# Each tile streams its own weights, with the two tiles in flight about a third of a layer apart

One step of a two-layer decoder, on the 8 NeuronCores of one Trainium2 chip. Each core computes one prompt sequence of 2048 tokens in four tiles of 512, and a sample group of 32 tokens. The metric is the device time of the slowest core, in microseconds.

## The reference

Cut to what matters: the residual stream passes four feed-forwards, a gated linear attention and a dilated window attention. All weights are shared by all tokens; only the recurrence's state and the keys and values go from tile to tile.

```python
# layer 0
x = x + 0.5 * swiglu_ffn(rmsnorm(x, g), w_in, w_out)      # 1024 -> 2*2688 -> 1024
x = x + gla_mixer(rmsnorm(x, g), ...)                     # recurrence over chunks of 64
x = x + 0.5 * swiglu_ffn(rmsnorm(x, g), w_in, w_out)
k, v = shared_kv(x, ...)                                  # k: per-head norm, rotary
# layer 1
x = x + 0.5 * swiglu_ffn(rmsnorm(x, g), w_in, w_out)
x = x + dilated_window_attention(q, k, v) @ w_o           # windows 128, 512, 2048
x = x + 0.5 * swiglu_ffn(rmsnorm(x, g), w_in, w_out)
```

## The kernel before

Weights come as units (fp32 in HBM, converted to bf16 on the way in) through one ring of 16,384 columns, eight units of 2048. A unit is free when all its users have used it: two prompt tiles, and in the first pass the sample tile. The program is written as Python threads; when it is built, a list scheduler with assumed times lays their instructions out in a fixed order for each engine. At run time each engine goes through its own list and waits for the others: on the slowest core before, TensorE's longest such wait in total is for a norm's VectorE outputs, 49.1 us in 16 waits.

```python
DMA_BW = 190e3
...
RING = 16384
ring = A("ring", [128, RING], BF16)
...
def add_unit(p, kind, i, src, n, users=0):                # p: pair of tiles
    u = Unit(src, n, users or (3 if p == 0 else 2), len(order))
...
def weights():
    for k, u in enumerate(order):
        if off + u.n > RING:
            off = 0
        lo, hi = off, off + u.n
        over = [(a, b, o) for (a, b, o) in live if a < hi and b > lo]
        yield need(lambda over=over: all(o.left == 0 for _, _, o in over))
        ...
        yield O(PL, (lambda e, u=u, dst=dst: e.dma_start(out=dst, in_=u.src)), ...)
...
# the scheduler: of the operations that can start about now, the one of lowest rank
m = min(c[0] for c in cands) + self.TIE
th = min((c for c in cands if c[0] <= m), key=lambda c: (c[1][0], c[1][1]))[1]
...
def c_act(n): return 0.11 + n * 0.00083                   # assumed ScalarE us
def c_dve(n, rate=1): return 0.07 + n / (960.0 * rate)    # assumed VectorE us
```

A feed-forward takes 21 units of the first projection ("wfi", 2048 columns, 16 matmuls for a tile) and 8 of the output projection ("wfo", 2688 columns, 21 matmuls).

Of the kernel before, what the change touches and what calls it, by code (L numbers as in the profile page):

```python
# [24 lines left out]
class Sched:  # L25
# [3 lines left out]
    DMA_BW = 190e3  # L29
# [117 lines left out]
class Threads:  # L147
# [10 lines left out]
    def spawn(self, gen, rank):  # L158
        self.seq += 1
        self.live.append([rank, self.seq, gen, None, None])  # L160

    def run(self):
        S = self.S
        while self.live:
            self.live.sort(key=lambda h: (h[0], h[1]))
            moved = False
            for th in list(self.live):
                while th[3] is None:
                    if th[4] is not None:
                        if not th[4]():  # L170
                            break
                        th[4] = None
                        moved = True
                    try:
                        item = next(th[2])
                    except StopIteration:
                        self.live.remove(th)
                        moved = True
                        break
                    moved = True  # L180
                    if item[0] == "op":
                        th[3] = item
                    else:
                        th[4] = item[1]
            cands = [(S.start_of(th[3][1], th[3][3], th[3][4]), th) for th in self.live if th[3] is not None]
            if not cands:
                if moved:
                    continue
                if self.live:
                    def where(g):  # L190
                        out = []
                        while g is not None:
                            if getattr(g, "gi_frame", None) is not None:
                                out.append("%s:%d" % (g.gi_code.co_name, g.gi_frame.f_lineno))
                            g = getattr(g, "gi_yieldfrom", None)
                        return " > ".join(out)
                    raise RuntimeError("deadlock of threads: %s" % [(h[0], where(h[2])) for h in self.live])
                break
            m = min(c[0] for c in cands) + self.TIE
            th = min((c for c in cands if c[0] <= m), key=lambda c: (c[1][0], c[1][1]))[1]  # L200
            _, eng, fn, reads, writes, cost, dma, nbytes = th[3]
            th[3] = None
            S.op(eng, fn, reads, writes, cost, dma, nbytes)
# [93 lines left out]
def build():  # L297
# [23 lines left out]
    RING = 16384  # L321
    ring = A("ring", [128, RING], BF16)
# [86 lines left out]

    units = {}  # L410
    order = []

    def add_unit(p, kind, i, src, n, users=0):
        u = Unit(src, n, users or (3 if p == 0 else 2), len(order))
        u.kind = kind
        units[(p, kind, i)] = u
        order.append(u)

    for p in range(2):
        def ffn_units(f, p=p):  # L420
            for j in range(NF):
                add_unit(p, "fi%d" % f, j, wfi[f * NF + j], 2048)
            for m in range(8):
                add_unit(p, "fo%d" % f, m, wfo[f * 8 + m], 2688)
        ffn_units(0)
        for gi, kind in enumerate(("v", "qk", "r", "o")):
            for i in range(4):
                add_unit(p, kind, i, wgl[gi * 4 + i], 2048)
            if p == 0 and kind == "qk":
                for s in range(4):  # L430
                    src = st_in[s * 4:(s + 1) * 4].rearrange("h p d -> p h d")
                    add_unit(0, "S0", s, src, 2048, 1)
                    add_unit(0, "S0b", s, src, 1024, 1)
        ffn_units(1)
        for i in range(2):
            add_unit(p, "kv", i, wkv[i], 2048)
        ffn_units(2)
        for i in range(3):
            add_unit(p, "wq", i, wqd[i], 2048)
        if p == 0:  # L440
            for s in range(4):
                add_unit(0, "ck", s, ck[s], 3328, 1)
                add_unit(0, "cv", s, cv[s], 3328, 1)
        for i in range(4):
            add_unit(p, "wo", i, wod[i], 1536)
        ffn_units(3)

    NWS = 12

    def weights():  # L450
        live = []
        off = 0
        for k, u in enumerate(order):
            if off + u.n > RING:
                off = 0
# [9 lines left out]
            if u.kind in ("S0", "S0b"):  # L465
                dst = dst.rearrange("p (h d) -> p h d", h=4)
            yield O(PL, (lambda e, u=u, dst=dst: e.dma_start(out=dst, in_=u.src)),  # L467
                    writes=[u.key] + [o.key for _, _, o in over], cost=1.0, dma="w%d" % (k % NWS), nbytes=u.n * 512)
            u.ready = True

    def use(T, kind, i):
        u = units[(T.p, kind, i)]
        yield need(lambda: u.ready)
        return u
# [16 lines left out]

    tiles = []
    for t in range(4):
        T = Tile()
        i = t % 2
        T.nm, T.i, T.p, T.t, T.n, T.rank = "t%d" % t, i, t // 2, t, 512, 10 * t
# [15 lines left out]
    TS.nm, TS.i, TS.p, TS.t, TS.n, TS.rank = "ts", "s", 0, -1, 32, -20  # L512
# [77 lines left out]
    def load_x(T, prev):  # L590
        nq = 4 if T.n == 512 else 1
        for q in range(nq):
            ms = range(q * 8 // nq, (q + 1) * 8 // nq)
            if prev is not None:
# [5 lines left out]
                writes=[xk(T, m) for m in ms], cost=0.1, dma="x%s_%d" % (T.b, q), nbytes=w * 512)  # L600
# [44 lines left out]
    def ffn(T, f, last):  # L645
# [14 lines left out]
        for j in range(NF):  # L660
# [8 lines left out]
            yield mm(g, [(v[:, kt, 0:128], T.h[:, kt, :]) for kt in range(8)], hks(T) + [u.key], bs[0], n)  # L669
            yield mm(up, [(v[:, kt, 128:256], T.h[:, kt, :]) for kt in range(8)], hks(T) + [u.key], bs[-1], n)  # L670
            u.left -= 1
            TH.spawn(post(j, bs, g, up), T.rank - 3)
# [7 lines left out]
        for m in range(8):  # L680
# [9 lines left out]
            TH.spawn(evac(m, b), T.rank - 4)  # L690
# [20 lines left out]
    def gla(T):  # L711
# [30 lines left out]
        TH.spawn(gate(), T.rank - 5)  # L742
# [5 lines left out]
        for hd in range(4):  # L748
            u = yield from use(T, "v", hd)
            v = u.ap.rearrange("p (kt c) -> p kt c", kt=8)  # L750
            for cp in range(2):
# [4 lines left out]
                TH.spawn(vpost(hd, cp, b, either()), T.rank - 3)  # L756
# [24 lines left out]
        for hd in range(4):  # L781
# [7 lines left out]
            TH.spawn(qkpost(hd, bs), T.rank - 4)  # L789
            if hd % 2:  # L790
                TH.spawn(recur(T, hd // 2), T.rank - 5)
# [39 lines left out]
        TH.spawn(rms_all(), T.rank - 5)  # L831
        for hd in range(4):
            u = yield from use(T, "r", hd)
            v = u.ap.rearrange("p (kt c) -> p kt c", kt=8)
            for f in range(2):
# [3 lines left out]
                TH.spawn(rpost(hd, f, b, i), T.rank - 4)  # L839
            u.left -= 1  # L840
        yield need(lambda: all(("u", T.nm, m) in done for m in range(8)))
        for q in range(4):
            u = yield from use(T, "o", q)
            v = u.ap.rearrange("p (kt c) -> p kt c", kt=8)
            for z in range(2):
# [4 lines left out]
                TH.spawn(resid(T, 2 * q + z, b, PS[b], n), T.rank - 4)  # L850
# [67 lines left out]
    def gla_s(T):  # L918
# [148 lines left out]
        for q in range(4):  # L1067
            u = yield from use(T, "o", q)
            v = u.ap.rearrange("p (kt c) -> p kt c", kt=8)
            for z in range(2):  # L1070
                (b,) = yield from get_banks(1)
                yield mm(PS[b][:, 0:n], [(v[:, kt, z * 128:(z + 1) * 128], uT[:, kt, :]) for kt in range(8)], [gk, u.key], b, n)
                TH.spawn(resid(T, 2 * q + z, b, PS[b][:, 0:n], n), T.rank - 4)
# [38 lines left out]
    def kv(T, tab):  # L1112
# [22 lines left out]
        for kc in range(2):  # L1135
            (b,) = yield from get_banks(1)
            yield mm(PS[b][:, 0:n], [(v[:, kt, kc * 128:(kc + 1) * 128], T.h[:, kt, :]) for kt in range(8)], h8 + [u.key], b, n)
            TH.spawn(kpost(kc, b), T.rank - 4)
# [38 lines left out]
        for bp in range(2):  # L1177
# [4 lines left out]
            TH.spawn(vpost(bp, b), T.rank - 4)  # L1182
        u.left -= 1

    def qproj(T, tab):
# [13 lines left out]
        for q in range(3):  # L1199
            u = yield from use(T, "wq", q)  # L1200
            v = u.ap.rearrange("p (kt c) -> p kt c", kt=8)
            for z in range(2):
                (b,) = yield from get_banks(1)
                yield mm(PS[b][:, 0:n], [(v[:, kt, z * 128:(z + 1) * 128], T.h[:, kt, :]) for kt in range(8)], hks(T) + [u.key], b, n)
                TH.spawn(qpost(2 * q + z, b), T.rank - 4)
# [5 lines left out]
    def attention(T):  # L1211
# [142 lines left out]
        for s in range(NW):  # L1354
            TH.spawn(worker(s, work[s::NW]), T.rank - 5 + 0.1 * s)
# [12 lines left out]
    def oproj(T):  # L1368
        n = T.n
        for q in range(4):  # L1370
            u = yield from use(T, "wo", q)
            v = u.ap.rearrange("p (kt c) -> p kt c", kt=6)
            for z in range(2):
                (b,) = yield from get_banks(1)
                yield mm(PS[b][:, 0:n], [(v[:, kt, z * 128:(z + 1) * 128], T.QT[:, kt, :]) for kt in range(6)], [rk(T, ("qt", c)) for c in range(6)] + [u.key], b, n)
                TH.spawn(resid(T, 2 * q + z, b, PS[b][:, 0:n], n), T.rank - 4)
# [75 lines left out]
    def tile_thread(T, prev):  # L1452
        T.sqn = 0
        yield from load_x(T, prev)
        yield from norm(T, 0)
# [21 lines left out]
    S.op(SP, lambda e: e.dma_start(out=CF[:], in_=cfd[:, :]), writes=["CF"], cost=0.1, dma="c0", nbytes=A_END * 512)  # L1477
    S.op(PL, lambda e: e.dma_start(out=CB[:], in_=cbd[:, :]), writes=["CB"], cost=1.0, dma="c1", nbytes=B_END * 512)
    TH.spawn(weights(), -30)

    def prologue():
        yield O(PL, lambda e: e.dma_start(out=WG2[:], in_=gg2[:, :]), [], ["WG2"], cost=1.0, dma="c2", nbytes=32768)
# [8 lines left out]
    TH.spawn(tile_thread(tiles[0], None), 0)  # L1491
    TH.spawn(tile_thread(TS, None), TS.rank)
    TH.spawn(tile_thread(tiles[1], None), 10)
    TH.spawn(tile_thread(tiles[2], tiles[0]), 20)
    TH.spawn(tile_thread(tiles[3], tiles[1]), 30)
# [86 lines left out]
```

## Time and profile before

| | before |
|---|---|
| time, median of 4 runs | 2614.62 us (2612.9 to 2615.6) |
| spans of the 8 cores in the profiled run | 2605.1 to 2607.7 us |
| TensorE busy, slowest core | 2365.2 us (91%) |
| weight queue | 169.75 MB written, HBM read 350 MB |

The page and the windows are read in the prediction. The slowest core is core 4. The page of core 0 says:

```profile
PE 2391.5 (92%) x14828; PEld 1165.2 (45%) x14828; DVE 1127.1 (43%) x2012; ACT 1197.5 (46%) x2312; POOL 171.0 (7%) x320
```

Its span is the same 2607.7 us.

### The profile page before, as it was taken

The numbers are of one execution on the slowest core, as the hardware profiler recorded it, in microseconds if no ns is written. First come the engines' busy times: TensorE is split into PE (matmuls) and PEld (weight loads), VectorE is DVE, ScalarE is ACT, GpSimd is POOL, SyncE is SP. The second block draws the span as 40 slices with busy tenths as digits, with TensorE's granted clock in tenths as the row PEclk, the third lists the DMA queues.
The fourth block names the chain that finished last, engine by engine and source line by source line (L and its number), as shares of the span: only waits on it lengthen the run. The fifth ranks groups of instructions, "written<-read, shape, count | busy, mean of one in ns | idle before, by whom it ended". The sixth has DMA issues, their size and how long they took to land.

```text
span 2607.7 us, 41140 instructions; the slowest of 8 cores (2605.1 to 2607.7 us)
## 1 busy us (share of the span) xinstructions
PE 2365.2 (91%) x14580; PEld 1164.6 (45%) x14828; DVE 1126.8 (43%) x2012; ACT 1197.6 (46%) x2312; POOL 171.0 (7%) x320
## 2 busy tenths in 40 slices
PE   1999997999989997699997999978999899976999
PEld 0444554444444444444443445543444444443444
DVE  1442356643265327554313333655434542565431
ACT  2553346555246525555404532665532453455540
POOL 1000010000000000100000000000000000000000
PEclk9999998999999998699998999999999999987999
DMA  7244336244455442734483443323545545311443
GB/s 143 41 65 75 60 67 112 50 73 73 70 95 89 81 74 44 116 59 77 81 165 79 71 80 67 61 45 63 89 78 95 89 81 90 61 33 33 76 94 86
DMA packets 62857, 200.90 MB, mean 77 GB/s; under 512 B 8080, under 2 KB 14912, under 8 KB 62528
## 3 DMA queue, kind: packets, MB, share of 16 engines
q0 software_dynamic: 45536, 169.75, 39.5%
q1 hardware_dynamic: 17120, 28.52, 3.6%
q8 instruction: 121, 1.98, 0.3%
q14 instruction: 80, 0.66, 0.1%
HBM read 350.47 MB, written 15.40 MB: 140 GB/s over the span
## 4 chain that ended last, share of the span: by engine, by line
PE 81%; DVE 7%; ACT 4%; issue 4%; DMA 2%; DVEq 0%; POOL 0%; ACTq 0%; SPq 0%; POOLq 0%
PE pst L565 78%; DVE h L581 3%; ACT p L570 2%; DMA ring<-wfi 2%; DVE r L578 1%; DVE p L578 1%; ACT h L570 1%; ACT r L574 1%; DMA x<-xp 1%; PE pst L1310 0%; PE pst L1249 0%; PE pst L1271 0%; PE pst L898 0%; DVE p L581 0%; PE pst L899 0%
## 5 line engine op out<-in xcount | busy, mean ns | idle before, releaser
L565 PE MATMUL pst<-h,ring 128*128 128x512 bf16 x5989 | 1358.0, 382 | 60.4 <-DVE h L581 45.8
L565 PEld LDWEIGHTS pst<-h,ring 128*128 128x128 bf16 x6144 | 596.4, 98 | 767.2 <-issue 83.6
L565 PE MATMUL pst<-r,ring 128*128 128x512 bf16 x3057 | 693.5, 382 | 28.4 <-DVE r L578 23.7
L570 ACT ACTIVATE p<-p 128x512 f32<-128x512 f32 x856 | 538.0, 629 | 86.2 <-DVE p L734 11.1
L578 DVE TENSOR_TENSOR p<-p,pst 128x512 f32<-128x512 f32 x368 | 252.4, 686 | 601.7 <-ACT p L570 596.4
L570 ACT ACTIVATE p<-pst 128x512 f32<-128x512 f32 (+1 forms) x472 | 279.1, 593 | 488.2 <-PE pst L565 473.4
L565 PEld LDWEIGHTS pst<-r,ring 128*128 128x128 bf16 x3136 | 303.6, 98 | 387.0 <-issue 37.5
L570 ACT ACTIVATE h<-x 128x512 bf16<-128x512 f32 x192 | 118.0, 626 | 464.0 <-DVE x L581 317.5
L578 DVE TENSOR_TENSOR r<-p,pst 128x512 bf16<-128x512 f32 x336 | 231.3, 688 | 60.6 <-DVE p L578 51.0
L581 DVE SCALAR_TENSOR_TENSOR x<-pst,x 128x512 f32<-128x512 f32 x128 | 87.9, 690 | 371.3 <-PE pst L565 361.4
L467 POOL DMA_DIRECT2D ring<-wfi x168 | 88.8, 531 | 1367.8 <-PE pst L565 1318.1
L581 DVE SCALAR_TENSOR_TENSOR h<-x,CF,p 128x512 bf16<-128x512 f32 x224 | 153.2, 746 | 54.0 <-ACT p L570 42.7
L565 PE MATMUL pst<-hsb,ring 128*128 128x32 bf16 x1536 | 53.7, 178 | 34.6 <-DMA ring<-wfi 34.6
L565 PE MATMUL pst<-h,CB 128*128 128x512 bf16 x184 | 52.6, 419 | 31.1 <-ACT h L570 26.3
L565 PE MATMUL pst<-ring,h 128*128 128x256 bf16 x640 | 77.8, 275 | 0.0
L565 PEld LDWEIGHTS pst<-hsb,ring 128*128 128x128 bf16 x1536 | 52.3, 97 | 55.3 <-issue 35.7
L467 POOL DMA_DIRECT2D ring<-wfo x64 | 33.8, 528 | 540.6 <-PE pst L565 540.6
L565 PEld LDWEIGHTS pst<-ring,h 128*128 128x128 bf16 x640 | 61.6, 99 | 11.6 <-issue 2.5
L570 ACT ACTIVATE spb<-pst 128x32 f32<-128x32 f32 (+2 forms) x111 | 21.6, 195 | 97.3 <-PE pst L565 95.5
L574 ACT COPY r<-pst 128x256 f32<-128x256 f32 (+3 forms) x104 | 50.6, 486 | 34.1 <-PE pst L774 14.5
L578 DVE TENSOR_TENSOR x<-x,pst 128x512 f32<-128x512 f32 x64 | 43.7, 686 | 49.6 <-PE pst L565 49.5
L570 ACT ACTIVATE spb<-spb 128x32 f32<-128x32 f32 (+2 forms) x194 | 44.9, 232 | 18.4 <-ACT spb L570 1.1
(145 smaller groups left out, 1067.1 us busy)
## 6 DMA issues: line engine op xcount, KB each, us to landing
ring<-wfi POOLq DMA_DIRECT2D x168, 512.0 KB, 5.7
ring<-wfo POOLq DMA_DIRECT2D x64, 672.0 KB, 7.1
ring<-wgl POOLq DMA_DIRECT2D x32, 512.0 KB, 6.5
x<-xp SPq DMA_DIRECT2D x16, 512.0 KB, 14.6
y_p<-x SPq DMA_DIRECT2D x32, 256.0 KB, 2.8
p<-rpd SPq DMA_DIRECT2D x16, 256.0 KB, 2.9
ring<-ck POOLq DMA_DIRECT2D x4, 832.0 KB, 9.3
ring<-cv POOLq DMA_DIRECT2D x4, 832.0 KB, 9.7
```

The lines of the kernel that those rows point to most:

```text
L467: yield O(PL, (lambda e, u=u, dst=dst: e.dma_start(out=dst, in_=u.src)), writes=[u.key] + [o.key for _, _, o in over], cost=1.0, dma="w%d" ...
L565: ins = e.matmul(out, lhsT=l, rhs=r, start=(start and i == 0), stop=(stop and i == last), skip_group_check=skip)
L570: return O(ACT, lambda e: e.activation(out=out, in_=in_, func=func, scale=scale, bias=bias), reads, writes, c_act(n))
L574: return O(ACT, lambda e: e.copy(out=out, in_=in_), reads, writes, c_act(n))
L578: return O(DVE, lambda e: e.tensor_tensor(out=out, in0=a, in1=b, op=op), reads, writes, c_dve(n, rate))
L581: return O(DVE, lambda e: e.scalar_tensor_tensor(out=out, in0=a, scalar=s, in1=b, op0=op0, op1=op1), reads, writes, c_dve(n))
```

## The change

The intent: as long as both tiles need the same unit, they must go through a layer in step, and meet their serial parts (norms, recurrence, attention) together. With own rings one tile can be in attention while the other fills TensorE with feed-forward. The lead is held by the rank: tile 0 has priority until it is 49,152 columns of weights ahead, then tile 1 has. (A tile's two layers have 307,200 columns, so this is about a third of one layer; where the prediction and I say "half a layer", this lead is meant.) The diff, cut to its core:

```diff
-    DMA_BW = 190e3
+    DMA_BW = 340e3
...
-            th = min((c for c in cands if c[0] <= m), key=lambda c: (c[1][0], c[1][1]))[1]
+            th = min((c for c in cands if c[0] <= m), key=lambda c: (c[1][0] + c[1][5](), c[1][1]))[1]
...
-    RING = 16384
-    ring = A("ring", [128, RING], BF16)
+    RING = 8192
+    rings = [A("ring%d" % i, [128, RING], BF16) for i in range(2)]
...
-    for p in range(2):
+    for t in range(4):
+        def add_unit(kind, i, src, n, users=0, t=t):
+            u = Unit(src, n, users or (1 if t else 2), (t, kind, i))
...
+    LEAD = 24 * 2048
+    def weights(slot):
+        if slot == 1:
+            yield need(lambda: S.lastw.get(("x", "b1", 7)) is not None)
...
     def use(T, kind, i):
+        if T.slot is not None:
+            prog[T.slot] += u.n
...
+        T.rank = (lambda i=i: 10 if i else 0 if prog[0] - prog[1] <= LEAD else 20)
...
     def load_x(T, prev):
+        if T.t == 1:
+            yield need(lambda: units[(0, "fi0", 3)].ready)      # and its DMA waits for that unit
...
+            if j == 0 and n == 512:                             # first unit: with the norm's outputs
+                for kt in range(8):
+                    for z, dst in ((0, g), (1, up)):
+                        yield mm(dst, ...)
...
     def prologue():
+        yield need(lambda: S.lastw.get(("x", "b0", 7)) is not None)
+        yield O(SP, lambda e: e.dma_start(out=CF[:], in_=cfd[:, :]), ...)   # gains, after x
```

More of the change, by code (lines that the diff above doesn't have):

```diff
@@ L156, in __init__, with spawn @@
         self.seq = 0
-    def spawn(self, gen, rank):
+    def spawn(self, gen, rank, base=None):
         self.seq += 1
-        self.live.append([rank, self.seq, gen, None, None])
+        self.live.append([rank, self.seq, gen, None, None, base or (lambda: 0)])
     def run(self):
@@ L164, in run @@
         while self.live:
-            self.live.sort(key=lambda h: (h[0], h[1]))
+            self.live.sort(key=lambda h: (h[0] + h[5](), h[1]))
             moved = False
@@ L410, in build, with ffn_units @@
     units = {}
-    order = []
-    def add_unit(p, kind, i, src, n, users=0):
-        u = Unit(src, n, users or (3 if p == 0 else 2), len(order))
-        u.kind = kind
-        units[(p, kind, i)] = u
-        order.append(u)
-    for p in range(2):
-        def ffn_units(f, p=p):
+    order = [[], []]
+    for t in range(4):
+        def add_unit(kind, i, src, n, users=0, t=t):
+            u = Unit(src, n, users or (1 if t else 2), (t, kind, i))
+            u.kind = kind
+            units[(t, kind, i)] = u
+            order[t % 2].append(u)
+        def ffn_units(f):
             for j in range(NF):
-                add_unit(p, "fi%d" % f, j, wfi[f * NF + j], 2048)
+                add_unit("fi%d" % f, j, wfi[f * NF + j], 2048)
             for m in range(8):
-                add_unit(p, "fo%d" % f, m, wfo[f * 8 + m], 2688)
+                add_unit("fo%d" % f, m, wfo[f * 8 + m], 2688)
         ffn_units(0)
@@ L427, in build @@
             for i in range(4):
-                add_unit(p, kind, i, wgl[gi * 4 + i], 2048)
-            if p == 0 and kind == "qk":
+                add_unit(kind, i, wgl[gi * 4 + i], 2048)
+            if t == 0 and kind == "qk":
                 for s in range(4):
                     src = st_in[s * 4:(s + 1) * 4].rearrange("h p d -> p h d")
-                    add_unit(0, "S0", s, src, 2048, 1)
-                    add_unit(0, "S0b", s, src, 1024, 1)
+                    add_unit("S0", s, src, 2048, 1)
+                    add_unit("S0b", s, src, 1024, 1)
         ffn_units(1)
         for i in range(2):
-            add_unit(p, "kv", i, wkv[i], 2048)
+            add_unit("kv", i, wkv[i], 2048)
         ffn_units(2)
         for i in range(3):
-            add_unit(p, "wq", i, wqd[i], 2048)
-        if p == 0:
+            add_unit("wq", i, wqd[i], 2048)
+        if t == 0:
             for s in range(4):
-                add_unit(0, "ck", s, ck[s], 3328, 1)
-                add_unit(0, "cv", s, cv[s], 3328, 1)
+                add_unit("ck", s, ck[s], 3328, 1)
+                add_unit("cv", s, cv[s], 3328, 1)
         for i in range(4):
-            add_unit(p, "wo", i, wod[i], 1536)
+            add_unit("wo", i, wod[i], 1536)
         ffn_units(3)
-    NWS = 12
-    def weights():
+    LEAD = 24 * 2048
+    NWS = 8
+    def weights(slot):
+        ring = rings[slot]
         live = []
         off = 0
-        for k, u in enumerate(order):
-            if off + u.n > RING:
+        if slot == 1:
+            yield need(lambda: S.lastw.get(("x", "b1", 7)) is not None)
+        for k, u in enumerate(order[slot]):
+            if off + u.n > RING or u.kind == "ck":
                 off = 0
@@ L467, in weights @@
             yield O(PL, (lambda e, u=u, dst=dst: e.dma_start(out=dst, in_=u.src)),
-                    writes=[u.key] + [o.key for _, _, o in over], cost=1.0, dma="w%d" % (k % NWS), nbytes=u.n * 512)
+                    [("x", "b1", 1)] if u.uid == (1, "fi0", 0) else [], writes=[u.key] + [o.key for _, _, o in over], cost=1.0, dma="w%d_%d" % (slot, k % NWS), nbytes=u.n * 512)
             u.ready = True
     def use(T, kind, i):
-        u = units[(T.p, kind, i)]
+        u = units[(T.u, kind, i)]
         yield need(lambda: u.ready)
+        if T.slot is not None:
+            prog[T.slot] += u.n
         return u
@@ L490, in build @@
     spool = Pool("spb", [spb[:, k, :] for k in range(10)])
+    prog = [0, 0]
     tiles = []
@@ L495, in build @@
         i = t % 2
-        T.nm, T.i, T.p, T.t, T.n, T.rank = "t%d" % t, i, t // 2, t, 512, 10 * t
+        T.nm, T.i, T.t, T.n = "t%d" % t, i, t, 512
+        T.rank = (lambda i=i: 10 if i else 0 if prog[0] - prog[1] <= LEAD else 20)
+        T.u, T.slot = t, i
         T.b = "b%d" % i
@@ L511, in build @@
     TS = Tile()
-    TS.nm, TS.i, TS.p, TS.t, TS.n, TS.rank = "ts", "s", 0, -1, 32, -20
+    TS.nm, TS.i, TS.t, TS.n, TS.rank = "ts", "s", -1, 32, (lambda: -20)
+    TS.u, TS.slot = 0, None
     TS.b = "bs"
@@ L599, in load_x @@
                 out=T.x[:, ms[0]:ms[-1] + 1, :].rearrange("p m n -> p (m n)"), in_=src[:, q * w:(q + 1) * w])),
-                writes=[xk(T, m) for m in ms], cost=0.1, dma="x%s_%d" % (T.b, q), nbytes=w * 512)
+                [units[(0, "fi0", 3)].key] if T.t == 1 else [], writes=[xk(T, m) for m in ms], cost=0.1, dma="x%s_%d" % (T.b, q), nbytes=w * 512)
             for m in ms:
@@ L668, in ffn @@
                 g, up = PS[bs[0]][:, 0:n], PS[bs[0]][:, n:2 * n]
-            yield mm(g, [(v[:, kt, 0:128], T.h[:, kt, :]) for kt in range(8)], hks(T) + [u.key], bs[0], n)
-            yield mm(up, [(v[:, kt, 128:256], T.h[:, kt, :]) for kt in range(8)], hks(T) + [u.key], bs[-1], n)
+            if j == 0 and n == 512:
+                for kt in range(8):
+                    for z, dst in ((0, g), (1, up)):
+                        yield mm(dst, [(v[:, kt, z * 128:(z + 1) * 128], T.h[:, kt, :])], [hk(T, kt), u.key], bs[z], n, start=(kt == 0), stop=(kt == 7))
+            else:
+                yield mm(g, [(v[:, kt, 0:128], T.h[:, kt, :]) for kt in range(8)], hks(T) + [u.key], bs[0], n)
+                yield mm(up, [(v[:, kt, 128:256], T.h[:, kt, :]) for kt in range(8)], hks(T) + [u.key], bs[-1], n)
             u.left -= 1
-            TH.spawn(post(j, bs, g, up), T.rank - 3)
+            TH.spawn(post(j, bs, g, up), -3, T.rank)
         yield need(lambda: all(("act", T.nm, f, j) in done for j in range(14)))
@@ L689, in ffn @@
             u.left -= 1
-            TH.spawn(evac(m, b), T.rank - 4)
+            TH.spawn(evac(m, b), -4, T.rank)
     def tail(T, m, last):
@@ L740, in gate @@
             pool.put("glr", gi)
-        TH.spawn(gate(), T.rank - 5)
+        TH.spawn(gate(), -5, T.rank)
         def vpost(hd, cp, b, eng):
@@ L755, in gla @@
                     yield mm(PS[b][:, a * 256:(a + 1) * 256], [(T.h[:, kt, c * 128:(c + 1) * 128], v[:, kt, :]) for kt in range(8)], h8 + [u.key], b, 256)
-                TH.spawn(vpost(hd, cp, b, either()), T.rank - 3)
+                TH.spawn(vpost(hd, cp, b, either()), -3, T.rank)
             u.left -= 1
@@ L788, in gla @@
             yield need(lambda: hd in gates)
-            TH.spawn(qkpost(hd, bs), T.rank - 4)
+            TH.spawn(qkpost(hd, bs), -4, T.rank)
             if hd % 2:
-                TH.spawn(recur(T, hd // 2), T.rank - 5)
+                TH.spawn(recur(T, hd // 2), -5, T.rank)
         rms = {}
@@ L829, in rms_all @@
                 yield from rmsq(hd)
-        TH.spawn(rms_all(), T.rank - 5)
+        TH.spawn(rms_all(), -5, T.rank)
         for hd in range(4):
@@ L838, in gla @@
                 yield mm(PS[b], [(v[:, kt, f * 128:(f + 1) * 128], T.h[:, kt, :]) for kt in range(8)], h8 + [u.key], b, n)
-                TH.spawn(rpost(hd, f, b, i), T.rank - 4)
+                TH.spawn(rpost(hd, f, b, i), -4, T.rank)
             u.left -= 1
@@ L849, in gla @@
                          [rk(T, ("u", kt)) for kt in range(8)] + [u.key], b, n)
-                TH.spawn(resid(T, 2 * q + z, b, PS[b], n), T.rank - 4)
+                TH.spawn(resid(T, 2 * q + z, b, PS[b], n), -4, T.rank)
             u.left -= 1
@@ L1072, in gla_s @@
                 yield mm(PS[b][:, 0:n], [(v[:, kt, z * 128:(z + 1) * 128], uT[:, kt, :]) for kt in range(8)], [gk, u.key], b, n)
-                TH.spawn(resid(T, 2 * q + z, b, PS[b][:, 0:n], n), T.rank - 4)
+                TH.spawn(resid(T, 2 * q + z, b, PS[b][:, 0:n], n), -4, T.rank)
             u.left -= 1
@@ L1137, in kv @@
             yield mm(PS[b][:, 0:n], [(v[:, kt, kc * 128:(kc + 1) * 128], T.h[:, kt, :]) for kt in range(8)], h8 + [u.key], b, n)
-            TH.spawn(kpost(kc, b), T.rank - 4)
+            TH.spawn(kpost(kc, b), -4, T.rank)
         u.left -= 1
@@ L1181, in kv @@
                 yield mm(PS[b][:, a * 256:(a + 1) * 256], [(T.h[:, kt, c * 128:(c + 1) * 128], v[:, kt, :]) for kt in range(8)], h8 + [u.key], b, 256)
-            TH.spawn(vpost(bp, b), T.rank - 4)
+            TH.spawn(vpost(bp, b), -4, T.rank)
         u.left -= 1
@@ L1204, in qproj @@
                 yield mm(PS[b][:, 0:n], [(v[:, kt, z * 128:(z + 1) * 128], T.h[:, kt, :]) for kt in range(8)], hks(T) + [u.key], b, n)
-                TH.spawn(qpost(2 * q + z, b), T.rank - 4)
+                TH.spawn(qpost(2 * q + z, b), -4, T.rank)
             u.left -= 1
@@ L1354, in attention @@
         for s in range(NW):
-            TH.spawn(worker(s, work[s::NW]), T.rank - 5 + 0.1 * s)
+            TH.spawn(worker(s, work[s::NW]), -5 + 0.1 * s, T.rank)
         yield need(lambda: left[0] == 0)
@@ L1375, in oproj @@
                 yield mm(PS[b][:, 0:n], [(v[:, kt, z * 128:(z + 1) * 128], T.QT[:, kt, :]) for kt in range(6)], [rk(T, ("qt", c)) for c in range(6)] + [u.key], b, n)
-                TH.spawn(resid(T, 2 * q + z, b, PS[b][:, 0:n], n), T.rank - 4)
+                TH.spawn(resid(T, 2 * q + z, b, PS[b][:, 0:n], n), -4, T.rank)
             u.left -= 1
@@ L1454, in tile_thread @@
         yield from load_x(T, prev)
+        yield need(lambda: "CF" in S.lastw)
         yield from norm(T, 0)
@@ L1474, in tile_thread @@
         yield from ffn(T, 3, True)
-    S.op(SP, lambda e: e.dma_start(out=CF[:], in_=cfd[:, :]), writes=["CF"], cost=0.1, dma="c0", nbytes=A_END * 512)
-    S.op(PL, lambda e: e.dma_start(out=CB[:], in_=cbd[:, :]), writes=["CB"], cost=1.0, dma="c1", nbytes=B_END * 512)
-    TH.spawn(weights(), -30)
+    S.op(PL, lambda e: e.dma_start(out=CB[:], in_=cbd[:, :]), [], ["CB"], cost=1.0, dma="c1", nbytes=B_END * 512)
+    TH.spawn(weights(0), -30)
+    TH.spawn(weights(1), -29)
     def prologue():
+        yield need(lambda: S.lastw.get(("x", "b0", 7)) is not None)
+        yield O(SP, lambda e: e.dma_start(out=CF[:], in_=cfd[:, :]), [], ["CF"], cost=0.1, dma="c0", nbytes=A_END * 512)
         yield O(PL, lambda e: e.dma_start(out=WG2[:], in_=gg2[:, :]), [], ["WG2"], cost=1.0, dma="c2", nbytes=32768)
@@ L1490, in build @@
     TH.spawn(prologue(), -25)
-    TH.spawn(tile_thread(tiles[0], None), 0)
-    TH.spawn(tile_thread(TS, None), TS.rank)
-    TH.spawn(tile_thread(tiles[1], None), 10)
-    TH.spawn(tile_thread(tiles[2], tiles[0]), 20)
-    TH.spawn(tile_thread(tiles[3], tiles[1]), 30)
+    for T, prev in ((tiles[0], None), (TS, None), (tiles[1], None), (tiles[2], tiles[0]), (tiles[3], tiles[1])):
+        TH.spawn(tile_thread(T, prev), 0, T.rank)
     TH.run()
```

## The prediction

> **What bounds the kernel now.** I read the page first, then the span in 40 windows, then the start in finer windows, then the chain of waits and who waited for whom on TensorE. The page:
>
> ```profile
> span 2607.7 us, 41140 instructions; the slowest of 8 cores (2605.1 to 2607.7 us)
> ...
> PE 2365.2 (91%) x14580; PEld 1164.6 (45%) x14828; DVE 1126.8 (43%) x2012; ACT 1197.6 (46%) x2312; POOL 171.0 (7%) x320
> ...
> PEclk9999998999999998699998999999999999987999
> DMA  7244336244455442734483443323545545311443
> ...
> q0 software_dynamic: 45536, 169.75, 39.5%
> q1 hardware_dynamic: 17120, 28.52, 3.6%
> ...
> HBM read 350.47 MB, written 15.40 MB: 140 GB/s over the span
> ...
> ring<-wfi POOLq DMA_DIRECT2D x168, 512.0 KB, 5.7
> ```
>
> TensorE is busy for 91% of the span; VectorE, ScalarE and the DMA engines are each under half. So TensorE's work is the floor, and what can be won is its idle time (2607.7 - 2365.2 = 242 us) and the time it ran at a low clock. HBM reads are twice the bytes that the weight queue writes, because weights are read as fp32 and written as bf16: a "512.0 KB" unit is 1 MB of reading. From the windows (name, then busy us and instructions of each engine, granted clock, DMA share, GB/s written):
>
> ```profile
> core 4: us, PE busy (x) PEld busy (x) DVE busy (x) ACT busy (x) POOL busy (x), PEclk, DMA share, GB/s
> 0.00:65.20 65.20, 11.77 (x151) 6.42 (x152) 8.78 (x32) 17.66 (x53) 8.04 (x18) 1.00 0.71 143
> ...
> 1043.20:1108.40 65.20, 42.13 (x711) 28.73 (x714) 36.33 (x75) 38.14 (x92) 8.35 (x15) 0.60 0.74 116
> ...
> 1369.20:1434.40 65.20, 47.23 (x197) 20.34 (x202) 25.38 (x38) 27.24 (x45) 2.64 (x5) 0.82 0.40 79
> ...
> 2086.40:2151.60 65.20, 64.88 (x298) 29.56 (x302) 26.15 (x38) 34.60 (x57) 4.75 (x9) 1.00 0.46 80
> ...
> 2347.20:2412.40 65.20, 42.26 (x383) 22.54 (x388) 36.42 (x63) 35.29 (x68) 2.11 (x4) 0.79 0.20 33
> ```
>
> The losses have three places. The first window leaves TensorE idle for 53.4 us. The feed-forward windows (2086) are full. The windows of attention (1043, 2347), of the gated recurrence and of the change of tiles (1369) lose 10 to 23 us each and run at a low clock, because both tiles share one ring, walk through the layer in step, and reach their serial parts together. Without start and end (6.3 us in the last window) the idle time is 242 - 53 - 6 = 183 us. Summing busy time times (1 - clock) over the 40 windows gives 78 us lost to the clock. TensorE's work at full clock is so about 2365 - 78 = 2287 us.
>
> ```profile
> 5.84 43.92 DMA ring<-wfi
> ...
> 1367.63 14.53 DMA x<-xp
> ```
>
> ```profile
> PE pst L565 <- DVE h L581: 49.1, 16, 12.6
> PE pst L565 <- DMA ring<-wfi: 36.4, 9, 5.9
> PE pst L565 <- ACT h L570: 26.3, 9, 16.9
> ```
>
> The chain starts with 44 us of weights and has 14.5 us of x at the change of tiles; the waits say that in between TensorE waits for the norm's VectorE and ScalarE steps, not for weights (all 36.4 us of that wait are in the start).
>
> [...] 64.88 us for 298 matmuls is 217.7 ns. [...] all eight cores have 1.00 in the window from 2086. [...] in stretches where the DMA engines are full:
>
> ```profile
> core 4: us, PE busy (x) PEld busy (x) DVE busy (x) ACT busy (x) POOL busy (x), PEclk, DMA share, GB/s
> 10.00:45.00 35.00, 3.90 (x104) 3.35 (x104) 3.64 (x20) 6.54 (x24) 0.00 (x0) 1.00 1.02 203
> ...
> 1055.00:1070.00 15.00, 8.47 (x149) 5.55 (x147) 8.40 (x16) 9.97 (x23) 0.59 (x2) 0.58 1.02 157
> ...
> 1376.00:1381.00 5.00, 0.00 (x0) 0.00 (x0) 0.00 (x0) 1.15 (x2) 0.00 (x0) 0.50 1.00 270
> ```
>
> Converted loads alone run at 157 GB/s written (157 to 167 on the eight cores in this window), some 320 read; x alone at 270. These are the figures that I use.
>
> **The change, part by part.**
>
> Matmuls: none added or removed (the instruction order has the same work in both). The floor stays 2287 us.
>
> Weights: each of four tiles now loads all of its own, where two tiles shared one load. A tile's weights are 307,200 columns of 128 partitions in bf16, 78.6 MB; four times that is 315 MB in place of 157 MB. Queue q0 so goes from 170 to about 327 MB. A unit of 512 KB now feeds 16 matmuls of one tile, 16 x 217.7 = 3.48 us, so dense TensorE needs 524,288 B / 3.48 us = 150.5 GB/s against the 160 that full DMA engines give: 94%. Whole run: 327 MB / 160 = 2044 us, and q1's 28.5 MB at 270 = 106 us, sum 2150 us of full DMA, against 2287 us of TensorE. So TensorE remains the bound, by 6%, and the rings (four units each) are what must carry every unevenness.
>
> Half a layer apart: the changed instruction order shows one tile's recurrence and attention laced with the other's feed-forward matmuls. By my count of that order, each attention stretch has 15 us of its own matmuls and 11 to 23 us of others; before, the last attention had 4 us of others. I expect two thirds of the 183 + 78 = 261 us to go, leaving about 85 us: dependent chains in four attentions and four recurrences at some 10 us each. This third is a judgement, from how tightly each chain waits.
>
> Start: the intent is that x comes first. But in the order of SyncE's queue, the first load of the second tile's x stands before two of the four loads of the first tile's x, and it waits for the fourth weight unit; behind it stand also the gains. Ahead of that unit come constants, four units and half an x: 6.0 MB of reading, at 320 GB/s some 19 us, so it lands near 22 us. Then come 3.5 MB of x and gains beside 4.2 MB for the second ring. The sum by the second tile's last x is again 13.7 MB, as before, so it lands near 49 us; and TensorE's order has the second tile's norm sums before the first tile's feed-forward. I put dense work at 53 us where it now starts at 66.6. The new alternation of the first unit's matmuls with the norm's outputs saves perhaps 3 of the 5.4 us that VectorE needs for eight. Idle at the start: 53 - 11 = 42 us in place of 53.
>
> End: the last tile runs alone for its lead, 49,152 of 307,200 columns, all in its feed-forward. That is dense alone, save that only three units of the output projection (672 KB) fit a ring and, after the switch of sizes, a unit is freed just one unit (21 x 0.218 = 4.6 us) before the next is needed, where one takes 7.1 us to land: two stalls of 2.5 us. End idle 6 + 5 = 11 us.
>
> Weights late in the middle: at 94% load with four units of buffer, x and y of each tile (4 MB, 15 us of DMA at 270 GB/s) must be caught up from 6% of slack, and loads of both rings share one queue on POOL in a fixed order. I put 25 us on it.
>
> Sum: 2287 + 42 + 85 + 25 + 11 = 2450 us.
>
> **The rivals.** (1) The DMA becomes the bound. For it: 94% in dense stretches; the mixture in the first 45 us (203 GB/s written) reads only some 300 GB/s, just the 301 that dense work needs; eight cores now draw that all the time. Against it: sample work (some 80 us) and norms, attention and recurrence (some 116 us, both my estimates from the groups' counts times durations) need few weights, so the DMA can catch up there. If the rate sinks to 145 GB/s written, the DMA needs 327 / 145 = 2255 us plus 106, and with start and end the time is 2420 at once with no other loss; with the chains on top 2500 to 2560. (2) The filling is near perfect: all but 30 us gone and the DMA keeps up. For it: ScalarE and VectorE are under half busy, and the order is laced finely. Then 2287 + 42 + 30 + 11 = 2370. (3) Static order turns on itself: matmuls of one tile stand behind the other's late ScalarE or VectorE result, as the fixed order of TensorE cannot step around it. For it: ScalarE's 629 ns for 512 columns is longer than the 535 that the kernel's scheduler assumes. Against: the same error is in the kernel now and its feed-forward windows are full. It would cost some 50 us: 2500.
>
> **Range and chances.** The sum is 2450. Filled as in (2) it is 2370, with DMA trouble as in (1) up to 2545. To stay within 2% (above 2562) most of the expected gain must be lost to the DMA; 9 in 100. Slower by 2% (above 2666) needs DMA rates below 140 GB/s for the whole run; 3 in 100. Faster by over 2%: 88.
>
> **What would show it.** Right: HBM reads near 665 MB, q0 near 327 MB, DMA digits 7 to 9 all along, PEclk digits 9 in the middle, no window with TensorE under 55 of 65 us but the first and the last, dense from some 53 us. Wrong in the DMA step: TensorE waiting for ring units for over 60 us after the start, DMA share at 1.00 in dense stretches below 150 GB/s. Wrong in the filling: waits for ScalarE and VectorE above 100 us. Wrong in the start: dense matmuls well before or after 53 us. A granted clock under 0.95 in dense stretches would break the floor itself.

The sum stands as 2287 + 42 + 85 + 25 + 11 = 2450 us; it uses the measured 217.7 ns for a matmul and 160 and 270 GB/s. The trace shows the clock that TensorE was granted: 0.50 from 1376 to 1391 us on core 4. That a low clock costs busy time times (1 - clock), as in the 78 us, I took as given. For 512-column matmuls in a row the trace shows it: on core 0 they follow each other after 427 ns at a granted 0.50 (448.3 to 452.6 us), and after 216 at 1.00. For the other matmuls I did not show it.

## The result, and the profile after

The changed kernel takes 2530.49 us in the median of 4 runs; three are fast (2524.0 to 2534.4), one is slow (2681.6, with a clock of 0.905 to 0.911 on one die) and is left out. Its ratio to the kernel before is 0.9671 (95% interval 0.9644 to 0.9697). Ratios are the mean time of one kernel's fast runs over that of the other's of the same rounds, so not quite the ratio of the quoted medians. The time lies in my range and is faster by over 2%, but it is 80 us above the 2450 that I named: only half of the forecast gain came.

From the page of the profiled run, slowest core:

```profile
span 2532.5 us, 42560 instructions; the slowest of 8 cores (2497.2 to 2532.5 us)
...
PE 2375.8 (94%) x14828; PEld 1146.6 (45%) x14828; DVE 1122.1 (44%) x2012; ACT 1198.3 (47%) x2312; POOL 319.9 (13%) x602
...
PEclk8999999999999998999999999999999999999999
DMA  7877787758878979976998978678689989598686
...
q0 software_dynamic: 86144, 327.05, 77.4%
...
HBM read 665.04 MB, written 15.40 MB: 269 GB/s over the span
```

The bytes are as worked out (327 and 665 MB). The clock row has no 6 and 7 in the middle any more, and 26 of core 7's 40 windows of 63 us are at 1.00. But TensorE's busy time is higher than on the page before, not lower, and the cores are spread over 35 us where it was 2.6.

Who waited for whom on TensorE, same run (total us, times, longest):

```profile
PE pst L579 <- ACT h L584: 36.3, 11, 24.7
PE pst L579 <- DMA ring<-wfo: 25.9, 20, 5.1
PE pst L579 <- DVE r L592: 21.0, 5, 7.0
PE pst L579 <- DMA ring<-wfi: 15.8, 18, 2.0
```

The wait for a norm's VectorE outputs (49.1 us before) is gone from the head of the list; most of the wait for ScalarE is the start. New are the waits for units: 47 us in all with 5.2 for the sample's cached values. I cut the lists of both kernels at 66 and 2440 us, to leave the start and the end out. Waits for VectorE and ScalarE fall from 161 to 50 us, and those for DMA rise from 2 to 42. So the lead works, and of the 111 us of waits that it took away 40 come back as waits for weights.

The start, in the timeline of TensorE (start, us, what, and the idle time ahead with its releaser):

```profile
37.04 3.15 PE L579 MATMUL pst<-h,CB 128*128 128x512 bf16 x7 [24.66 <-ACT h L584]
42.29 1.79 PE L579 MATMUL pst<-hsb,ring 128*128 128x32 bf16 x64 [2.10 <-DVE hsb L595]
43.92 0.59 PE L579 MATMUL pst<-h,CB 128*128 128x512 bf16 x1
54.44 3.20 PE L579 MATMUL pst<-h,CB 128*128 128x512 bf16 x8 [9.93 <-ACT h L584]
57.48 8.80 PE L579 MATMUL pst<-h,ring 128*128 128x512 bf16 x40
```

and of SyncE's queue:

```profile
1.50 24.23 SPq L614 DMA_DIRECT2D x<-xp  x6
25.78 1.01 SPq L1506 DMA_DIRECT2D CF<-cfd  x1
```

That is as forecast: the six x issues hang on the fourth unit until 25 us, the gains come behind, and the first tile's feed-forward starts only after the second tile's norm sums, at 57 us (54 with those sums) where I said 53.

### The profile page after: what moved, and what is told of

Same layout as the page of the kernel before. It is cut to its first block, busy times and chain, and to the rows that moved or that the text cites. A ratio compares the mean times of both kernels' runs of the same rounds, so it can differ in the third digit from the quotient of the medians.

```text
span 2532.5 us, 42560 instructions; the slowest of 8 cores (2497.2 to 2532.5 us)
## 1 busy us (share of the span) xinstructions
PE 2375.8 (94%) x14828; PEld 1146.6 (45%) x14828; DVE 1122.1 (44%) x2012; ACT 1198.3 (47%) x2312; POOL 319.9 (13%) x602
## 3 DMA queue, kind: packets, MB, share of 16 engines
q0 software_dynamic: 86144, 327.05, 77.4%
## 4 chain that ended last, share of the span: by engine, by line
PE 72%; DMA 15%; ACT 4%; DVE 4%; issue 3%; SPq 0%; POOL 0%; ACTq 0%; DVEq 0%; POOLq 0%
PE pst L579 69%; DMA ring<-wfi 6%; DMA ring<-wfo 6%; ACT p L584 2%; DVE h L595 2%; DMA x<-xp 1%; DMA ring<-wgl 1%; DMA kp<-p 1%; DVE p L592 1%; DMA ring<-cv 1%; ACT h L584 1%; DVE r L592 1%; DMA vp<-p 1%; PE pst L1332 0%; ACT Sbf L926 0%
## 5 line engine op out<-in xcount | busy, mean ns | idle before, releaser
L579 PE MATMUL pst<-h,ring 128*128 128x512 bf16 x6144 | 1388.0, 381 | 7.0 <-DMA ring<-wfi 2.8
L579 PE MATMUL pst<-r,ring 128*128 128x512 bf16 x3136 | 720.5, 385 | 37.7 <-DVE r L592 20.4
L475 POOL DMA_DIRECT2D ring<-wfi x336 | 177.5, 529 | 1194.8 <-PE pst L579 1080.1
L475 POOL DMA_DIRECT2D ring<-wfo x128 | 67.6, 529 | 545.4 <-PE pst L579 462.1
L475 POOL DMA_DIRECT2D ring<-wgl x64 | 33.8, 529 | 271.2 <-PE pst L579 245.2
L588 ACT COPY r<-pst 128x512 f32<-128x512 f32 (+3 forms) x104 | 50.6, 486 | 14.8 <-PE pst L1360 6.4
```

What stands on the lines that cost most here:

```text
L579: ins = e.matmul(out, lhsT=l, rhs=r, start=(start and i == 0), stop=(stop and i == last), skip_group_check=skip)
L588: return O(ACT, lambda e: e.copy(out=out, in_=in_), reads, writes, c_act(n))
```

## The experiments

Differences are taken from 2530 us. The three fast runs of the changed kernel have a mean of 2528.3 and four more on another chip 2529.9, so a difference is sure to some 2 us at best. Waits "in the middle" are those between 66 and 2440 us on the slowest core.

Two theories on the 80 us. FLOOR: the waits were about right, and TensorE's own work is 60 to 80 us more than the 2287 that I took. DMA: the crowded transfers stretch the whole run, also in gaps too short to be listed. Twelve kernels ran, one of them the changed kernel again, and all computed the right result except the two that halve the weights. Edits are against the changed kernel.

**Half of the weight bytes.** The instruction order stays; the result is wrong.

```diff
+            sr = u.src
+            if k >= 4 and ...:                # all but units that follow state or cache data
+                dst, sr = dst[:, 0:u.n // 2], u.src[:, 0:u.n // 2]
```

> The changed kernel with the same instruction order, but nearly every weight unit loads only its first half (the second half keeps older weights, so the result is wrong on purpose): the weight queue should move some 180 MB in place of 327. Theory FLOOR (the waits I forecast were about right, but TensorE's own work is some 60 to 80 us more than I took): only the waits for weights (43 us in the middle, some 7 at the end) and the spread of 35 us between the cores go, so 2455 to 2480 us, and TensorE stays busy for 2345 us or more. Theory DMA (crowded DMA engines stretch the whole run, also in gaps too short to be listed as waits): 2430 us or less, and TensorE's busy time falls below 2330.

Measured: fast runs 2473 us (2472.1 to 2475.7), ratio 0.944. The page of its slowest core:

```profile
span 2471.3 us, 42560 instructions; the slowest of 8 cores (2458.8 to 2471.3 us)
...
PE 2356.9 (95%) x14828; PEld 1148.0 (46%) x14828; DVE 1122.4 (45%) x2012; ACT 1197.0 (48%) x2312; POOL 319.8 (13%) x602
```

The waits for DMA in the middle fall from 42 to 6.5 us, the spread of the profiled run from 35 to 12.5 us, and the time by 57 us. TensorE stays busy for 2357 us. So the doubled traffic costs 57 us, and even without it the kernel stays 23 us above my 2450, though I had counted 25 us of late weights in that: FLOOR holds. DMA in its strong form falls. Its weak form does not: TensorE's busy time falls too, by 16 to 23 us on the four cores that have all records in both runs (1, 3, 5, 7), besides the listed waits.

**A lead of 0.** Own rings, tiles in step.

```diff
-    LEAD = 24 * 2048
+    LEAD = 0 * 2048
```

> The changed kernel with a lead of 0 columns in place of 49,152: own rings, but the two tiles in step. Theory OFFSET: the half layer between them is what fills the gaps, so waits for VectorE and ScalarE in the middle go back from 50 to 110 us or more and the time is 2580 to 2620. Rival: own rings are enough, as the scheduler fills gaps with whatever is ready: 2520 to 2545.

Measured: 2628 us, ratio 1.003 (0.998 to 1.009), a little past what OFFSET allows. Waits for VectorE and ScalarE in the middle are 117 us, with the waits for weights still 43; the granted clock is back at 0.96. From the waits of its slowest core:

```profile
PE pst L579 <- ACT p L584: 25.2, 20, 9.1
PE pst L579 <- ACT h L584: 24.1, 9, 19.1
PE pst L579 <- DMA ring<-wfo: 21.3, 16, 3.7
```

So own rings without the lead win nothing: against the kernel before, 44 us less of waits for VectorE and ScalarE stand against 41 us more for weights. The lead is worth 98 us.

**The start mended.** All of the first tile's x and the gains ahead of the second tile's x in SyncE's queue; the second tile's norm after the first tile's fourth unit.

```diff
-            yield need(lambda: units[(0, "fi0", 3)].ready)
+            yield need(lambda: units[(0, "fi0", 3)].ready and S.lastw.get(("x", "b0", 7)) is not None)
...
         yield need(lambda: "CF" in S.lastw)
+        if T.t == 1:
+            yield need(lambda: prog[0] >= 4 * 2048)
```

> The changed kernel with the start mended: all of the first tile's x and the gains stand before the second tile's x in SyncE's queue, and the second tile's norm waits until the first tile has taken four units. Theory ORDER (the misplaced wait and TensorE's order cost the start): dense matmuls from 30 to 38 us in place of 54 to 57, and the time falls by 15 to 22 us, to 2508 to 2515. Rival (the 13.7 MB that must land first set the start, in whatever order): dense work starts earlier but starves for units, the time falls by under 6 us.

Measured: 2522 us, 8 us less, between the two. The feed-forward starts at 35 us, 22 earlier, but then:

```profile
35.24 16.40 PE L579 MATMUL pst<-h,ring 128*128 128x512 bf16 x63 [4.12 <-DVE h L595]
51.47 1.67 PE L579 MATMUL pst<-h,CB 128*128 128x512 bf16 x7
57.59 0.59 PE L579 MATMUL pst<-hsb,ring 128*128 128x32 bf16 x16 [4.45 <-DMA ring<-wfi]
```

After the first four units TensorE waits 4.5 us for the fifth, which stands behind 2 MB of the second tile's x and 4 MB for its ring. In this run the waits for units (wfi and wfo) are 47.5 us over the whole run, against 41.7. Waits in the first 66 us fall by 14.5 us, and about half of that reaches the time.

**The start spread.** Gains first, the second tile's x behind units 5, 8, 11 and 14 of the first tile, its ring behind units 15 to 18, its norm after the 18th.

```diff
+            if T.t == 1:
+                yield need(lambda: units[(0, "fi0", 5 + 3 * q)].ready)
...
+            first = u.uid[:2] == (1, "fi0") and u.uid[2] < 4
+            if first:
+                yield need(lambda: units[(0, "fi0", 15 + u.uid[2])].ready)
```

> The changed kernel with the start mended and spread: gains first, the first tile's x next, the second tile's x one load at a time behind the first tile's units 5, 8, 11 and 14, its ring behind units 15 to 18, its norm after the first tile's 18th unit. Theory SPREAD (the first mend gained only 8 us because 6.3 MB for the second tile landed on top of the first tile's units): dense from 28 to 36 us and no wait of over 3 us for a unit between 36 and 110, so 2500 to 2512 us. Rival (the start is bound by bytes whatever their order): not under 2517.

Measured: 2524 us (fast runs 2519.0 to 2524.4), so the theory SPREAD falls, and the rival's number holds: dense only from 38 us, and units are late by 3.2 us at 67. Its windows:

```profile
20.00:30.00 10.00, 1.18 (x32) 1.02 (x32) 1.01 (x6) 2.53 (x10) 0.00 (x0) 1.00 0.67 147
30.00:40.00 10.00, 5.77 (x14) 1.77 (x15) 3.21 (x6) 3.35 (x7) 0.00 (x0) 1.00 0.00 1
```

From 30 to 40 us the DMA is idle (share 0.00), as the ring of the first tile is full and the second tile's loads are held back. Yet waits in the first 66 us fall by 16 us (32.6 in place of 48.7), those in the middle stay (92 and 91), and the profiled runs differ by just that (2519.0 and 2534.4). The means of the fast runs differ by 6 to 8 us only. The fast runs of either kernel lie 5 to 10 us apart, so how much of the 16 us is kept stays open, and what the idle stretch cost no run shows.

**Assumed times set to measured ones.** Only the scheduler's model.

```diff
-    DMA_BW = 340e3
+    DMA_BW = 315e3
-    return 0.11 + n * 0.00083
+    return 0.17 + n * 0.0009
-    return 0.07 + n / (960.0 * rate)
+    return 0.15 + n / (960.0 * rate)
```

> The changed kernel, only the scheduler's assumed times set to what the traces show (512 columns: ScalarE 630 ns in place of 535, VectorE 683 in place of 603; reads at 315 GB/s in place of 340), which alters the static order. Theory STATIC ORDER (TensorE waits because its fixed order was laid out for engines that are too fast): 15 to 35 us less, 2495 to 2515. Rival (the order hardly matters, the waits are those of dependent chains and weights): within 8 us of 2530.

The page before has 629 ns for ScalarE's 512 columns, and for VectorE's 686 to 690, with 746 for the norm's outputs. (The 683 of the expectation is what the new formula gives.)

Measured: 2503 us (2493.8 to 2503.6), 27 us less: STATIC ORDER holds. Waits in the middle fall from 91 to 78 us and TensorE's busy time from 2376 to 2364 on the slowest cores; the two together give 25 of the 27 us. So my rival (3), which I gave little weight, has part in what was left. How much is not shown: the DMA rate was changed with the two engines' times, and of the 14 us of waits 9 are for VectorE and ScalarE and 5 for weights. Nor did I try another order with wrong times, so part of the gain may be the luck of one order.

**Output-projection units on a grid.**

```diff
+            if u.kind.startswith("fo"):
+                off = (off + 2687) // 2688 * 2688
```

> The changed kernel, only with the output-projection units laid on a grid of 2688 columns, so that the third of them does not wait for the first. Theory SWITCH (the waits for output-projection units, 26 us of which 6 at the end, come from the change of unit size in a ring of three): those waits fall under 12 us and the time by 8 to 18 us, 2512 to 2522. Rival (they come from crowded DMA engines): within 6 us of 2530.

Measured: 2516 us, 14 us less, as SWITCH says, but its reason holds for the end alone: after 2440 us the waits for those units fall from 7.5 to 0.8 us, while in the middle they stay (18.4 and 19.3), so in all they fall from 25.9 to 20.1 and not under 12. Those for first-projection units fall from 15.8 to 7.0. The cause of this second part stays open.

**Rings of three units.**

```diff
-    RING = 8192
+    RING = 6656
```

> The changed kernel with rings of 6,656 columns in place of 8,192: three units of the first projection, two of the output projection. Theory DEPTH (at 94% of the DMA rate it is the ring's depth that hides a transfer): waits for weights in the middle rise from 42 to over 150 us and the time to over 2640. Rival (the rate alone counts): under 2560.

Measured: 2577 us from two fast runs, 47 more. Both expectations miss. The waits for weights in the middle hardly rise (48 in place of 42 us), far from DEPTH's 150. Over the whole run those for projection units rise by 24 us (from 41.7 to 66.1), 14 of it outside the middle, so a shorter ring does cost waits for the ring. Besides, waits for VectorE in the middle are 54 in place of 37 us and the clock is 0.975, in a static order that the scheduler laid out anew for the smaller ring.

**Three mends together** (assumed times, spread start, grid).

> Three mends together: the scheduler's assumed times, the spread start and the grid. If they add up: 27 + 22 + 10 us off 2530, so 2465 to 2478. If they share the same waits (weights late at 94% of the DMA rate): 2485 to 2500. TensorE stays busy for 2345 to 2370 us, by the theory FLOOR.

Measured: fast runs 2479, 2482 and 2491 us, ratio 0.948 to the kernel before. The mean of 2484 falls between my two forecasts. The first took 22 and 10 us for the spread start and the grid, which had not run yet; with the parts as they were then measured (27, 7 and 14 us) the sum is 2482, so within the noise they add up. It beats both kernels.

**The lead on top of the three mends.** These ran on another chip, where the kernel before had no run under 2639 us (five of seven were slow), so ratios to it mislead. I compare with the changed kernel, which ran beside them:

> The changed kernel itself, unaltered, as the yardstick on the same chip: 2520 to 2540 us, ratio 0.963 to 0.971.

It took 2530 us, as on the first chip.

```diff
-    LEAD = 24 * 2048
+    LEAD = 36 * 2048        # and 12 * 2048
```

> The three mends with a lead of 36 units (73,728 columns) in place of 24. If the lead is past its knee: within 10 us of 2486. If the second tile's attention still meets the first's late steps: 2465 to 2476, with the waits for VectorE in the middle (22 us) under 12.

> The three mends with a lead of 12 units. A lead of 0 cost the unmended kernel 98 us. If the gain grows steadily with the lead, half of it is lost here: 2520 to 2545. If a lead of one mixer's length (16 units of the recurrence's weights) is what counts, most of it is lost: over 2545. If a small lead is enough: under 2505.

Measured: 2558 us with 36 units, 2493 us with 12. With 36 both forecasts were wrong; with 12 the last of the three holds, that a small lead is enough. More lead is worse by some 74 us, with 90 us of waits for VectorE and ScalarE in the middle in place of 37 and a clock near 0.966; half the lead is nearly as good as 24. So the gain does not grow with the distance. That it depends on which serial part meets which is my guess; which parts meet at 36 I did not trace.

**Three mends with half of the bytes.**

> The three mends with half of nearly every weight unit (wrong result on purpose). Theory FLOOR: TensorE's busy time stays between 2340 and 2365 us on the cores with all records, and the time falls by what is left of waits for weights (34 us in the middle, 15 in the start and end) and of the spread between the cores: 2415 to 2440. If it goes under 2400, TensorE's own work is less than I now hold.

Measured: fast runs 2430.6, 2440.3 and 2441.9 us. TensorE is busy for 2343 to 2352 us on the six cores whose traces have all records. FLOOR holds, with the time at the upper edge of its range (mean 2437.6, two runs just past 2440), and weights still cost the best version some 46 us (against the mean of 2484.0, on another chip).

## Why the prediction was right in kind and half right in size

Every step by its own number, slowest core of the profiled runs:

| step | predicted us | measured us |
|---|---|---|
| TensorE's work, with the third of the clock loss that was to stay | 2287 + 26 = 2313 | 2375.8 |
| idle in the start | 42 | 48.7 |
| idle in the middle, chains | 59 (the rest of the 85) | 49.7 (waits for VectorE and ScalarE) |
| weights late in the middle | 25 | 41.6 |
| idle at the end | 11 | 13.6 |
| idle that no list names | none | 3.1 |
| sum | 2450 | 2532.5 |

**The step that failed is the floor**, as the prediction put it: "TensorE's work at full clock is so about 2365 - 78 = 2287 us." It carries 63 of the 82 us, from three sources.

The 2365 was read from a trace with 248 matmul records missing; with all of them core 0 has 2391.5 us, 26 more. The two counts stood side by side in the very line that I quoted. (The 217.7 ns that I took for a matmul has the same fault; core 0 has 303 in that window, 215 ns each.)

The 78 us for the clock were summed over windows of 65 us. A mean clock over such a window mixes TensorE's busy time with its idle gaps, in which the clock can be low: it was 0.50 from 1376 to 1381 us, where TensorE did nothing. Over all of core 0's time (1 - clock) sums to 116 us before and 36 after, and 44 and 9 of it fell on idle time. With windows of 1 us the sum of busy time times (1 - clock) is 56 us on core 4 and 72 on core 0. Busy time less this sum is an estimate of the work at full clock. On the five cores summed with all records (0, 1, 3, 5, 7) it is 2320 to 2326 us, 33 to 39 more than 2287. The windows make 22 us of that (2365 - 56 = 2309 on core 4), the rest goes with the missing records.

And the work seems to have grown. By the same estimate it is 2338 to 2342 us on these cores after the change, some 17 more, beside 27 to 36 us lost to the clock where I had left 26. On core 7, the slowest, the misreading is 35 us of the 63, the growth 18 and the clock 10. For core 0, which has all records in both runs, busy time went from 2391.5 to

```profile
PE 2365.0 (94%) x14828; PEld 1145.8 (46%) x14828; DVE 1123.0 (45%) x2012; ACT 1197.7 (48%) x2312; POOL 320.5 (13%) x602
```

that is by 26.5 us. Its costliest groups before:

```profile
L565 PE MATMUL pst<-h,ring 128*128 128x512 bf16 x6144 | 1379.2, 384 | 50.4 <-DVE h L581 46.1 <-DVE spb L578 2.5 <-ACT p L570 1.2
L565 PE MATMUL pst<-r,ring 128*128 128x512 bf16 x3136 | 703.5, 383 | 24.5 <-DVE r L578 24.5
```

and after:

```profile
L579 PE MATMUL pst<-h,ring 128*128 128x512 bf16 x6144 | 1381.6, 380 | 4.6 <-DVE h L595 2.2 <-DVE r L592 0.9 <-ACT p L584 0.6
L579 PE MATMUL pst<-r,ring 128*128 128x512 bf16 x3136 | 717.3, 384 | 29.9 <-DVE r L592 20.1 <-DMA ring<-wfo 9.4 <-DMA ring<-wod 0.4
```

Everything outside these two groups (recurrence, attention, norms) became 42.7 us cheaper, and the two dense groups 16 us dearer. This split is not one of clock against bytes: with a lead of 0, at the same bytes, core 1's two groups take 2062 us and the rest 340, against 2106 and 266 with the lead. Halving the bytes in the same order isolates what they add to the busy time: on core 1 it takes off 19 us (2371.4 to 2352.1), of it 11 in the output projections, 3 in the first group and 5 elsewhere; on core 3 18 us. The estimated work at full clock falls to 2330 to 2332 us, so the bytes make about half of its growth, and the clock takes the rest of the 19. The other half stays open; it may be that busy time outside the 512-column matmuls does not stretch in full with the clock, so that the estimate takes off too much before the change. (With half of the bytes, near the traffic before, the sum of busy time times (1 - clock) falls from 69 to 20 us on core 1, but busy time by 37 only, 2389.5 to 2352.1.) A matmul's record lasts 380 ns where the next followed after 215 in dense stretches, so by my estimate (380 - 215) a stall of up to some 165 ns is counted as busy; that the bytes act through such short stalls is my reading.

**What was right.** The mechanism: the lead is what wins (98 us when taken away). The bytes, to the megabyte. The start, at 54 to 57 us where I said 53, with its cause in the order of SyncE's queue and of TensorE; two mends of just these moved it. The end, whose stalls after the switch of unit sizes the grid took away (7.5 to 0.8 us). TensorE stayed the bound and the DMA the next, at 77% of the span for the weight queue. The total idle time, 137 forecast (163 less the 26 of clock) and 157 measured. That the chains came to 50 us and not 59 owes something to luck: the third was a judgement, and it was taken of 183 us of idle time, of which the profile lists 163 as waits; most of the rest were missing records.

**What was mis-sized besides.** Late weights cost 42 us in the middle and not 25. And I had no term for the spread: the time is that of the slowest of eight cores, which now stands 14 us above their median (2519 us) where it stood 1 us above. (This is not a further term of the table, which is for the slowest core.) In the fast runs the cores are 22 to 35 us apart, with half of the bytes 10 to 18, so the bytes make a good part of it.

**Of the rivals**, (1) was near in size (DMA trouble to 2545) but not in kind, since the rate did not sink below the 160 GB/s that I took: 327.05 MB in 77.4% of 2532.5 us is 167 GB/s. (3) has part in the 27 us that the run with measured times won; (2) fell.

## What to carry to other kernels

Before a busy time is taken as a floor, compare the count of matmuls with that of weight loads, and take a core that has all records (26 us here); and weigh busy time by the clock in windows short enough that idle gaps do not count (56 us on core 4 in place of 78). Letting two streams of work run out of step paid here (98 us), but its price was the shared fetch (57 us), and the distance has to be tried: 12 and 24 units were good here, 0 and 36 were not. The static order depended on its assumed times: setting three of them to what the trace shows won 27 us here, with no other edit.
